# Moving the split weights to other byte offsets in SBUF

## The chip, the cores and the metric

The kernel runs on one core of a Trainium2 chip. The metric is the device time of one execution in microseconds (us). An instruction's duration is given in nanoseconds (ns). The engines are named as the profile names them: PE is the matrix engine (its weight loads are listed apart, as PEld), DVE the vector engine, ACT the scalar engine, POOL the GpSimd engine, and SP the engine that issues most of the transfers.

## What is computed

One layer of a transformer block on 512 rows of 1024 features, in float32: half a SwiGLU feed-forward added to the input, then a token mixer (four heads of differential attention and eight heads of dilated attention), then another half feed-forward, and a last normalisation.

```python
x = x + 0.5 * swiglu(rmsnorm(x, ffn1_norm), ffn1_w_gate, ffn1_w_up, ffn1_w_down)
x = x + token_mixer(rmsnorm(x, mix_norm), w_in, w_out, ...)
x = x + 0.5 * swiglu(rmsnorm(x, ffn2_norm), ffn2_w_gate, ffn2_w_up, ffn2_w_down)
return rmsnorm(x, final_norm)
```

The hidden width of the feed-forward is 2816, which is 22 blocks of 128. `w_in` is 1024 x 3072 (queries, keys and values of both kinds of heads), `w_out` is 1024 x 1024.

## The kernel before, in words

Activations are kept transposed: a tile has 128 features as partitions and the 512 rows as columns. PE multiplies in a format with fewer bits than float32 (fp32r), so each operand is split into a high and a low part, and `mm3` (lines 122 to 125) issues three matmuls for one product: high weight by high activation (line 123), high weight by low activation (line 124), low weight by high activation (line 125). Every matmul loads its stationary operand, 128 columns of 4 bytes, with a load of its own (LDWEIGHTS), and then streams its moving operand of 512 or 256 columns.

The split weights lie in one tile `w_all` of 6 x 1024 floats and a few more (line 100). `w_place(shift)` (line 103) deals out three places in turn: place i has its high part at column 1024 i + shift and its low part 3072 columns further on. `load_w` fetches raw weights into one of three `raw` buffers and takes a place. `split_w`, or `high` and `low`, then fill it: ACT casts the raw weights to the high part, DVE subtracts to get the low part. The program's framework makes each writer wait until the last matmul that read any column it overwrites has finished.

Three kinds of work use the places.

- Plain units: gate and up blocks at the start of each feed-forward, and the first six blocks of each down product. Their shift is 0, the matmuls are 512 columns wide, and the weights are the stationary operand.
- Units of seven products (function `pipeline` in `ffn`): the rest of the gate, up and down products is done two blocks by two, with seven products of half-size blocks in place of eight. Their shift is `ODD`, which is 8 floats or 32 bytes (the inner `high`, line 376). One product is twelve matmuls of 256 columns, the weights are the stationary operand, and the moving tiles start at multiples of 256 bytes. The first feed-forward has 23 such units and the second 25, so there are 48 x 7 = 336 products, or 4032 matmuls. Their order on PE, ACT and DVE is set by a heap of due times with a fixed step of 1410 ns for a product (`STEP`).
- The mixer: `load` (line 849) calls `load_w` with shift 0. Query and key products (`pq`, `pk`: 384 matmuls) and the output product (`pwo`: 192) stream 512 columns of activations over stationary weights. The value product (`pv`, lines 896 to 898: 384 matmuls) is the other way round: the activations are stationary, and 256 columns of the weights are the moving operand.

In the built program `w_all` starts at a multiple of 256 bytes, and so do all activation tiles. Therefore both operands of a value matmul start at the same place within 256 bytes, and the weights of a seven-product matmul stand 32 bytes past its moving operand. The three `raw` buffers, the first input tile and the small tiles are allocated behind `w_all`.

In the mixer the order on PE, ACT and DVE is written out by hand in chunks, with score, transpose and value work of the attention set between them. The output product is the end of the mixer: `wo_mm(m, ks)` multiplies output block m for the feature blocks `ks`. Blocks 3 to 7 are done whole, one after the other (line 1195), each in the order of k from 0 to 7, and `wo_end(m)` adds the result to the residual. The second feed-forward begins with plain units, whose weights (`raw_gub`) are split while the last output blocks are multiplied.

Of the kernel before, what the change touches and what calls it, by code (L numbers as in the profile page):

```python
# [15 lines left out]
F32R = mybir.dt.float32r  # L16
# [5 lines left out]
P = 128  # L22
# [3 lines left out]
KD = D // P  # L26
# [27 lines left out]

STEP, PLAIN_STEP = 1410, 4080
HS = S // 2
ODD = 8
F32_MAX = 3.4028234e38
PSUM = bass.MemoryType.PSUM
DRAM = bass.MemoryType.DRAM  # L60
# [4 lines left out]
def tile_macaron(ctx: ExitStack, tc, xs, xT, wf, wgu1, wst1, wd1, wdg1, wqk, wv, wo, wgu2, wst2, wd2,  # L65
# [8 lines left out]
    wp = ctx.enter_context(tc.tile_pool(name="wp", bufs=3))  # L74
# [7 lines left out]
    def mm_bank(nm):  # L82
        return pp.tile([P, S], F32, tag="mm", name=nm, bufs=4)
# [13 lines left out]

    w_all = wp.tile([P, 6 * 1024 + ODD], F32R, tag="w", name="w", bufs=1)  # L100
    w_used = [0]

    def w_place(shift=0):
        o = w_used[0] % 3 * 1024 + shift
        w_used[0] += 1
        return w_all[:, o:o + 1024], w_all[:, 3072 + o:4096 + o]

    def load_w(src, nm, n=1024, shift=0):
        raw = wp.tile([P, 1024], F32, tag="raw", name=f"raw_{nm}")
        nc.sync.dma_start(raw[:, :n], src)  # L110
        return (raw, *w_place(shift))
# [10 lines left out]
    def mm3(po, wh, wl, mh, ml, first, last, on=False):  # L122
        T.matmul(po, wh, mh, start=first, stop=False, skip_group_check=on)  # L123
        T.matmul(po, wh, ml, start=False, stop=False, skip_group_check=on)  # L124
        T.matmul(po, wl, mh, start=False, stop=last, skip_group_check=on)  # L125
# [72 lines left out]
    def ffn(wgu, wst, wd, wdg, n0, n1, norm, early, res, nm, hooks, ended, first=None,  # L198
# [169 lines left out]
        def high(t):  # L368
# [5 lines left out]
            else:  # L374
                if not half:
                    h, l = w_place(ODD)
                    half.extend([(h[:, :512], l[:, :512]), (h[:, 512:], l[:, 512:])])
# [231 lines left out]
        def pipeline():  # L609
            seen = {}  # L610
            for t, (u, o) in enumerate(ops):
                if o[0] == "p":
                    at(starts[t] - 2 * PLAIN_STEP, 1, load, u)
                    at(starts[t] - 3 * STEP, 3, high, t)
                    at(starts[t] - 2 * STEP, 2.5, low, t)
                else:
                    if t == begin[u]:
                        if u != units[0]:

                            time, s0 = starts[t] - 14 * STEP, sum_slots(u)  # L620
                            if s0 in seen:
                                time = max(time, starts[begin[seen[s0]] + 2])
                            seen[s0] = u
                            if u == ("g", PLAIN + 10):


                                time += STEP
                            at(time, 1, weight_sums, u)
                        at(starts[t] - 7 * STEP, 1.5, load, u)
                    if o[0] in ("s2", "s4"):  # L630
                        at(starts[t] - 5 * STEP, 2, total, t)
                    at(starts[t] - 4 * STEP, 3, high, t)
                    at(starts[t] - 3 * STEP, 2.5, low, t)
                at(starts[t], 4, product, t)
# [75 lines left out]
    with tc.manual_schedule(engines={mybir.EngineType.DVE, mybir.EngineType.Activation}):  # L710
        for t in range(4):
            raw = wp.tile([P, 1024], F32, tag="raw", name=f"raw_f{t}")
            h, l = w_place()
            for kk in range(2):
                k = 2 * t + kk
# [17 lines left out]
                for j in range(2):  # L733
                    for c in range(2):
                        o = kk * 512 + (2 * j + c) * P
# [104 lines left out]
    units, chunks = [], []  # L840
# [6 lines left out]
    loaded, ready, later = {}, {}, []  # L847

    def load(n):
        if n < len(units) and n not in loaded:  # L850
            loaded[n] = load_w(*units[n])
            ready[n] = loaded[n][1:]

    def high(n, c):
# [8 lines left out]
    def prep(n, now=False):  # L863
        if n >= len(units):
            return
        load(n)
        for c in (0, 512):
            if now:
                split_w(*loaded[n], c, c + 512)
            else:  # L870
                later.append((lambda c=c: high(n, c), lambda c=c: low(n, c)))
# [108 lines left out]
    mh, ml = [None] * KD, [None] * KD  # L980
# [147 lines left out]
    wo_ps = {}  # L1128

    def wo_mm(m, ks):  # L1130
        wh, wl = ready[wo_units[m]]
        for k in ks:
            o = k * P
            mm3(wo_ps[m][:], wh[:, o:o + P], wl[:, o:o + P], mh[k][:], ml[k][:],
                k == 0, k == KD - 1)

    def wo_chunk(m, c):
        if c == 0:
            if m + 2 < WO:
                prep(wo_units[m] + 2)  # L1140
            wo_ps[m] = mm_bank(f"pwo{m}")
        wo_mm(m, range(2 * c, 2 * c + 2))

    for m in range(WO):
        chunks += [lambda m=m, c=c: wo_chunk(m, c) for c in range(3)]
    chunks += [lambda m=m: wo_mm(m, [KD - 2]) for m in range(WO)]

    means, spread = rstd("n2", held)
# [31 lines left out]
    def wo_end(m):  # L1180
        V.tensor_tensor(x[m], wo_ps[m][:], x[m], op=ALU.add)
        split_x(m, 2, early[0][m], early[1][m])
        square_x(m)

    early = early_x("b")
    for m in range(WO):
        wo_mm(m, [KD - 1])
# [3 lines left out]
    for m in range(WO, KD):  # L1191
        if m > WO:
            prep(wo_units[m], True)
        wo_ps[m] = mm_bank(f"pwo{m}")
        wo_mm(m, range(KD))
        wo_end(m)

    eps = sp.tile([P, 1], F32, tag="eps", name="eps", bufs=1)
# [172 lines left out]
```

## Time and profile before

| | |
|---|---|
| median of three runs | 949.8 us (949.75 to 950.12) |
| span of the profiled execution | 950.1 us |
| PE busy | 934.4 us, 98% |
| weight loads busy | 866.6 us, 91% |
| DVE busy | 724.2 us, 76% |
| ACT busy | 533.0 us, 56% |

The profile gives the span of the profiled execution from its first to its last instruction; it gives no other time of that execution. A matmul's listed duration contains the time until its last result has left the array, which overlaps the next matmuls; the spacing from one start to the next is what a matmul costs. The first feed-forward's units of seven products run from about 84 to 349 us, the mixer from 349 to 598 us, and the second feed-forward from there to about 933 us.

### The profile page before, as it was taken

The numbers are of one execution on the slowest core, as the hardware profiler recorded it, in microseconds if no ns is written. First come the engines' busy times: TensorE is split into PE (matmuls) and PEld (weight loads), VectorE is DVE, ScalarE is ACT, GpSimd is POOL, SyncE is SP. The second block draws the span as 40 slices with busy tenths as digits, with TensorE's granted clock in tenths as the row PEclk, the third lists the DMA queues.
The fourth block names the chain that finished last, engine by engine and source line by source line (L and its number), as shares of the span: only waits on it lengthen the run. The fifth ranks groups of instructions, "written<-read, shape, count | busy, mean of one in ns | idle before, by whom it ended". The sixth has DMA issues, their size and how long they took to land.

```text
span 950.1 us, 17200 instructions
## 1 busy us (share of the span) xinstructions
PE 934.4 (98%) x6452; PEld 866.6 (91%) x6452; DVE 724.2 (76%) x1490; ACT 533.0 (56%) x1102; POOL 98.2 (10%) x117
## 2 busy tenths in 40 slices
PE   9999999999999999999999999999999999999995
PEld 7789999999999998988989888889999899999995
DVE  6697897777997896669764537697899677798786
ACT  7454664455664665566756645455666344666462
POOL 0011101012102100000000003201110111220100
PEclk9999999999999999999999999999999999999997
DMA  7176646578757642443232204454673857874732
GB/s 249 62 202 153 156 128 177 143 192 204 189 147 184 180 129 67 132 134 117 83 113 89 67 23 133 132 148 119 157 205 89 209 142 181 223 190 118 194 106 89
DMA packets 60388, 136.71 MB, mean 144 GB/s; under 512 B 6848, under 2 KB 9152, under 8 KB 60304
## 3 DMA queue, kind: packets, MB, share of 16 engines
q1 hardware_dynamic: 46304, 110.14, 35.3%
q0 software_dynamic: 14000, 25.47, 17.1%
q8 instruction: 50, 0.82, 0.4%
q14 instruction: 34, 0.28, 0.1%
HBM read 130.30 MB, written 2.14 MB: 139 GB/s over the span
## 4 chain that ended last, share of the span: by engine, by line
PE 91%; DVE 5%; ACT 1%; issue 1%; DMA 1%; SPq 0%; DVEq 0%
PE po L1038 2%; PE pwo L123 1%; PE pwo L124 1%; PE pwo L125 1%; PE pua L123 1%; PE pua L124 1%; PE pua L125 1%; PE pv L898 1%; PE pv L896 1%; PE pv L897 1%; PE pt L1025 1%; PE pq L123 1%; PE pq L125 1%; PE pq L124 1%; PE pdb L125 1%; PE pdb L124 1%
## 5 line engine op out<-in xcount | busy, mean ns | idle before, releaser
L1004 DVE CUSTOM_DVE_ANT_0 pr<-sc,strip 128x128 f32<-128x128 f32 (+3 forms) x64 | 30.9, 488 | 35.1 <-PE sc L1002 34.8
L1007 ACT ACTIVATE pr<-pr,mx 128x128 f32<-128x128 f32 (+3 forms) x64 | 36.0, 563 | 32.5 <-DVE mx L1004 31.6
L382 ACT CAST w<-s2b 128x512 fp32r<-128x512 f32 x50 | 31.0, 620 | 17.6 <-DVE s2b L364 14.4
L386 DVE TENSOR_TENSOR w<-s2b,w 128x512 fp32r<-128x512 f32 x50 | 34.2, 685 | 8.0 <-ACT w L382 7.9
L382 ACT CAST w<-s2a 128x512 fp32r<-128x512 f32 x46 | 28.6, 621 | 18.7 <-DVE s2a L364 15.7
L1038 PEld LDWEIGHTS po<-v,ptb 128*128 128x128 f32 x240 | 32.8, 191 | 5.3 <-ACT ptb L1028 2.7
L150 POOL TENSOR_TENSOR sq<-sq,sqt 128x512 f32<-128x512 f32 x7 | 10.9, 1557 | 254.7 <-ACT sqt L149 254.7
L386 DVE TENSOR_TENSOR w<-s2a,w 128x512 fp32r<-128x512 f32 x46 | 31.5, 684 | 6.6 <-ACT w L382 6.5
L896 PE MATMUL pv<-w,xh 128*128 128x256 f32 x128 | 36.2, 283 | 0.0
L898 PE MATMUL pv<-w,xh 128*128 128x256 f32 x128 | 36.2, 283 | 0.0
L897 PE MATMUL pv<-w,xl 128*128 128x256 f32 x128 | 36.2, 282 | 0.0
L1038 PE MATMUL po<-v,ptb 128*128 128x64 f32 (+1 forms) x240 | 32.6, 269 | 1.8 <-ACT ptb L1028 1.7
L1028 ACT COPY ptb<-pt 128x128 f32<-128x128 f32 (+3 forms) x48 | 20.1, 424 | 20.2 <-PE pt L1025 19.9
L123 PE MATMUL pq<-xh,w 128*128 128x512 f32 x64 | 26.9, 421 | 0.0
L123 PE MATMUL pwo<-mh,w 128*128 128x512 f32 x64 | 26.1, 408 | 0.0
L124 PE MATMUL pwo<-ml,w 128*128 128x512 f32 x64 | 25.5, 398 | 0.0
L125 PE MATMUL pwo<-mh,w 128*128 128x512 f32 x64 | 25.5, 398 | 0.0
L124 PE MATMUL pq<-xl,w 128*128 128x512 f32 x64 | 25.1, 393 | 0.0
L123 PE MATMUL pk<-xh,w 128*128 128x512 f32 x64 | 25.1, 392 | 0.0
L125 PE MATMUL pq<-xh,w 128*128 128x512 f32 x64 | 25.1, 392 | 0.0
L125 PE MATMUL pk<-xh,w 128*128 128x512 f32 x64 | 25.0, 391 | 0.0
L124 PE MATMUL pk<-xl,w 128*128 128x512 f32 x64 | 25.0, 390 | 0.0
(661 smaller groups left out, 3990.0 us busy)
## 6 DMA issues: line engine op xcount, KB each, us to landing
raw_qk<-wqk_dram SPq DMA_DIRECT2D x16, 512.0 KB, 3.3
raw0bg<-wst_dram SPq DMA_DIRECT2D x9, 512.0 KB, 4.5
raw_gua<-wgu_dram SPq DMA_DIRECT2D x8, 512.0 KB, 3.9
raw0ag<-wst_dram SPq DMA_DIRECT2D x8, 512.0 KB, 4.7
raw0ad<-wdg_dram SPq DMA_DIRECT2D x8, 512.0 KB, 4.5
strip<-bias_rows SPq DMA_DIRECT2D x16, 256.0 KB, 3.6
raw_v<-wv_dram SPq DMA_DIRECT2D x8, 512.0 KB, 3.3
raw_wo<-wo_dram SPq DMA_DIRECT2D x8, 512.0 KB, 3.2
```

Source lines behind the costliest of these rows:

```text
L123: T.matmul(po, wh, mh, start=first, stop=False, skip_group_check=on)
L124: T.matmul(po, wh, ml, start=False, stop=False, skip_group_check=on)
L125: T.matmul(po, wl, mh, start=False, stop=last, skip_group_check=on)
L382: A.copy(made[t][0], source(t))
L386: V.tensor_tensor(l, source(t), h.bitcast(F32), op=ALU.subtract)
L896: T.matmul(po, xh[k][:, xs], wh[:, o:o + 256], start=k == 0, stop=False)
L897: T.matmul(po, xl[k][:, xs], wh[:, o:o + 256], start=False, stop=False)
L898: T.matmul(po, xh[k][:, xs], wl[:, o:o + 256], start=False, stop=k == KD - 1)
L1004: V.tensor_tensor_reduce(out=pi, in0=ps[:, :w], in1=st["b"][m][:, w - 1::-1], op0=ALU.add, op1=ALU.min, scale=1.0, scalar=3.0e38, accum_ou ...
L1007: A.activation(pi, pi, AF.Exp, scale=-1.0, bias=st["mx"][:, m, i:i + 1], accum_out=st["ls"][:, m, i:i + 1])
L1028: A.copy(ptb[:, :w], pt[:, :w])
L1038: T.matmul(st["po3"][:, i, d0:d0 + dn], st["ptb", m, i][:, k * P:(k + 1) * P], vt[u // 4, k][:, fo + d0:fo + d0 + dn], start=k == 0, stop= ...
```

## The change

The shift of the units of seven products goes from 8 to 13 floats (52 bytes), and the mixer's units get a shift of 51 floats (204 bytes, which is 52 short of 256). `w_all` grows by 43 floats. The last output block goes through k from 7 to 0 in place of 0 to 7; which matmul opens and which closes the sum in PSUM is set accordingly.

```diff
-ODD = 8
+ODD = 13
+MIX = 51
...
-    w_all = wp.tile([P, 6 * 1024 + ODD], F32R, tag="w", name="w", bufs=1)
+    w_all = wp.tile([P, 6 * 1024 + MIX], F32R, tag="w", name="w", bufs=1)
...
     def load(n):
         if n < len(units) and n not in loaded:
-            loaded[n] = load_w(*units[n])
+            loaded[n] = load_w(*units[n], shift=MIX)
...
     def wo_mm(m, ks):
         wh, wl = ready[wo_units[m]]
-        for k in ks:
+        for n, k in enumerate(ks):
             o = k * P
-            mm3(wo_ps[m][:], wh[:, o:o + P], wl[:, o:o + P], mh[k][:], ml[k][:],
-                k == 0, k == KD - 1)
+            first, final = (n == 0, n == KD - 1) if len(ks) == KD else (k == 0, k == KD - 1)
+            mm3(wo_ps[m][:], wh[:, o:o + P], wl[:, o:o + P], mh[k][:], ml[k][:], first, final)
...
-        wo_mm(m, range(KD))
+        wo_mm(m, range(KD)[::-1] if m == KD - 1 else range(KD))
```

In the built program the tiles behind `w_all` move up by 192 bytes (the `raw` buffers from 32 to 224 bytes past a multiple of 256). The matmuls on PE are the same and stand in the same order, but for the last output block. On ACT and DVE the same instructions stand in another order at two places: at the beginning of the mixer the first two casts of `raw_qk` stand behind the last copy of `pyda`, and at its end the two first splits of `raw_gub` change places, so that the one which overlaps the last 51 columns of the last output block's weights comes second.

## The prediction

> **What bounds the kernel now.** I read the page's shares first, then the chain that ended last, then busy time by stage, and then single matmuls, because the change touches only where their operands lie.
>
> ```profile
> span 950.1 us, 17200 instructions
> ...
> PE 934.4 (98%) x6452; PEld 866.6 (91%) x6452; DVE 724.2 (76%) x1490; ACT 533.0 (56%) x1102; POOL 98.2 (10%) x117
> ...
> PEclk9999999999999999999999999999999999999997
> ...
> PE 91%; DVE 5%; ACT 1%; issue 1%; DMA 1%; SPq 0%; DVEq 0%
> ```
>
> PE is busy 98% of the span and is 91% of the chain. The granted clock is full nearly everywhere, so the throttle is no part of this. The windows by stage (first feed-forward's units of seven products, mixer, second feed-forward) say where PE has slack:
>
> ```profile
> 84.00:349.00 265.00, 264.70 (x2088) 257.27 (x2087) 216.09 (x402) 153.45 (x309) 37.65 (x45) 1.00 0.65 167
> 349.00:598.00 249.00, 245.64 (x1491) 217.25 (x1490) 158.60 (x433) 145.79 (x353) 9.12 (x6) 0.99 0.31 98
> 598.00:933.00 335.00, 335.00 (x2474) 319.24 (x2473) 271.46 (x503) 186.77 (x365) 45.16 (x51) 1.00 0.60 155
> 700.00:740.00 40.00, 40.00 (x340) 40.00 (x339) 35.13 (x67) 25.46 (x54) 3.48 (x4) 1.00 0.50 132
> ```
>
> The columns are the window, its length, and busy us of PE, PEld, DVE, ACT and POOL. PE has 0.3, 3.4 and 0.0 us of idle time in the three stages. So what one matmul costs is paid in full, times the number of matmuls. The busiest stretch of DVE that I looked at has it at 35.13 of 40 us; it has room for a PE that is some per cent faster.
>
> **What one matmul costs now.** The spacing of starts is the cost. From the timeline of PE, three pairs of rows: a stretch of products of seven (the second row is 120 matmuls after the first), a value product (16 after), and the last output block with the first matmul behind it (24 after).
>
> ```profile
> 178.67 0.28 PE L123 MATMUL pxda<-h5a,w 128*128 128x256 f32 x1
> ...
> 192.87 0.28 PE L123 MATMUL pxda<-h5a,w 128*128 128x256 f32 x1
> ```
> ```profile
> 362.80 0.28 PE L898 MATMUL pv<-w,xh 128*128 128x256 f32 x1
> ...
> 364.72 0.28 PE L896 MATMUL pv<-w,xh 128*128 128x256 f32 x1
> ```
> ```profile
> 592.28 0.39 PE L123 MATMUL pwo<-mh,w 128*128 128x512 f32 x1
> ...
> 597.72 0.39 PE L123 MATMUL pgb<-ehb,w 128*128 128x512 f32 x1
> ```
>
> 14.20 us / 120 = 118.3 ns in the products of seven; 1.92 us / 16 = 120.0 ns in the value product; 5.44 us / 24 = 226.7 ns at 512 columns. The first two have the same shape, 128x128 weights and 256 columns. They differ by 1.7 ns, in every such stretch, as the groups show:
>
> ```profile
> L124 PE MATMUL pwgb<-xl,w 128*128 128x256 f32 x72 | 20.2, 281 | 0.0
> L898 PE MATMUL pv<-w,xh 128*128 128x256 f32 x128 | 36.2, 283 | 0.0
> L125 PE MATMUL pk<-xh,w 128*128 128x512 f32 x64 | 25.0, 391 | 0.0
> ```
>
> The listed duration is the spacing plus about 163 ns (281 against 118.3, 283 against 120.0), so differences of durations are differences of cost. Per operation, with least, median and largest duration:
>
> ```profile
> L124 PE MATMUL pwgb<-xl,w x72: 277/281/285, 654.1 to 868.7; 128*128 128x256 f32 x72
> ...
> L125 PE MATMUL pk<-xh,w x64: 388/389/398, 349.7 to 536.5; 128*128 128x512 f32 x64
> ```
> ```profile
> L898 PEld LDWEIGHTS pv<-w,xh x128: 187/192/192, 362.0 to 516.9; 128*128 128x128 f32 x128
> L898 PE MATMUL pv<-w,xh x128: 278/283/288, 362.1 to 517.0; 128*128 128x256 f32 x128
> ```
>
> In the products of seven the offset between the two operands is 32 bytes (modulo 256), in the value product it is 0. The weight loads differ too: 192 ns at offset 0, against 188 in the products of seven:
>
> ```profile
> L124 PEld LDWEIGHTS pwgb<-xl,w x72: 187/188/191, 654.0 to 868.6; 128*128 128x128 f32 x72
> ```
>
> I read this as the load of the next weights and the stream of this matmul getting into each other's way, more at offset 0 than at 32.
>
> **The change part by part.**
>
> *Products of seven, 32 to 52 bytes.* 48 units x 7 products x 12 = 4032 matmuls. No row has an offset of 52. Bounds: if every one took the least duration (277 in place of 281) the stage would win 4 x 4032 = 16.1 us, if every one took the largest (285) it would lose 16.1 us. I take the slope between the two offsets that the trace has: 1.67 ns for 32 bytes, so another 1.04 ns for 20 bytes. That is 4032 x 1.04 = 4.2 us less, a spacing of 117.3 ns.
>
> *Value product, weights 0 to 204 bytes.* Here the weights are the moving operand. The stationary tile is then 204 bytes behind, which modulo 256 is 52 ahead, the same relation as above. By the same slope 52 x 0.052 = 2.7 ns; 384 x 2.7 = 1.0 us less. Bounds: least 278 against 283, 1.9 us less; largest 288, 1.9 us more. The stage has PE idle of 3.4 us in all, so most of it reaches the end.
>
> *Query, key and output products, 0 to 204 bytes at 512 columns.* 384 + 192 matmuls. The load is done well inside the stream of 512 columns. Taken at 0; bounds from the key row: least 388 against a mean of 391, 576 x 3 = 1.7 us less; largest 398, 4.0 us more.
>
> *Casts and subtractions to the new places, raw buffers 192 bytes higher.* Taken at 0, because the offsets of the trace make no difference to them and PE covers them:
>
> ```profile
> L382 ACT CAST w<-s2b 128x512 fp32r<-128x512 f32 x50 | 31.0, 620 | 17.6 <-DVE s2b L364 14.4 <-PE pyub L125 1.4 <-PE pdb L125 1.0
> L114 ACT CAST w<-raw_qk 128x512 fp32r<-128x512 f32 x4 | 2.5, 620 | 1.9 <-DVE lp L806 0.9 <-PE pwda L124 0.5 <-ACT w L382 0.5
> ```
>
> The first writes 32 bytes past, the second 0, both 620 ns. If they grew 5%, DVE would stand at 36.9 of 40 us in the window above, still behind PE.
>
> *Seam into the mixer.* A place at shift 51 covers the head of the next place, so the casts of `raw_qk` wait for three more matmuls (3 x 118 = 0.35 us), and the first one also stands behind the copy of `pyda`.
>
> ```profile
> 342.97 0.62 ACT L114 CAST w<-raw_qk 128x512 fp32r<-128x512 f32 x1 [0.45 <-ACT w L382]
> 343.50 0.37 ACT L411 COPY pyda<-pxda 128x256 f32<-128x256 f32 x1
> 344.40 0.63 ACT L114 CAST w<-raw_qk 128x512 fp32r<-128x512 f32 x1 [0.53 <-PE pwda L124]
> 345.97 0.62 ACT L114 CAST w<-raw_qk 128x512 fp32r<-128x512 f32 x1 [0.95 <-DVE lp L806]
> ...
> 349.81 0.62 ACT L787 ACTIVATE sqd<-x 128x512 f32<-128x512 f32 x1
> ```
> ```profile
> 348.52 0.40 PE L123 MATMUL pq<-xh,w 128*128 128x512 f32 x1
> ```
>
> The first query matmul starts at 348.52, over 4 us after the first cast, so it doesn't wait. Queued behind the third cast on ACT are a table load and the squares (349.81) that the normalisation of the mixer waits for; these may come up to 0.35 us later, and the chain goes through them. I take 0.3 us more, with 0 and 0.4 as ends.
>
> *Seam into the second feed-forward.* Its first split (`raw_gub`) now overlaps the last 51 columns of the last output block, so it must wait for block k = 7. The reversed order of k puts that first: three matmuls, until 592.28 + 0.68 = 592.96 (without the reversal: 597.72, a stall of PE for the cast). ACT casts both `raw_gub` tiles from 592.25 on, 1.05 us each, DVE subtracts at 1.23 each:
>
> ```profile
> 592.25 1.05 ACT L114 CAST w<-raw_gub 128x1024 fp32r<-128x1024 f32 x1 [3.24 <-PE pwo L124]
> ```
> ```profile
> 593.33 1.23 DVE L115 TENSOR_TENSOR w<-raw_gub,w 128x1024 fp32r<-128x1024 f32 x1 [0.17 <-ACT w L114]
> ```
>
> Done by about 595.9, before PE wants them at 597.72: 0 us.
>
> ```profile
> 587.89 1.23 DVE L115 TENSOR_TENSOR w<-raw_gub,w 128x1024 fp32r<-128x1024 f32 x1 [0.17 <-ACT w L114]
> ```
> ```profile
> 603.13 1.05 ACT L114 CAST w<-raw_gub 128x1024 fp32r<-128x1024 f32 x1 [3.24 <-PE pub L124]
> ```
>
> The buffer of the first tile is free now when its subtraction ends, at 589.1, and will be at 595.9, so the load after it is issued that much later. The cast that this load serves is the fourth and starts at 603.13; I take the 7 us left as enough.
>
> **Sum** against the profiled execution: 950.1 - 4.2 - 1.0 + 0.3 = 945.2. Its span is 0.3 us over the median of the runs, so 944.9 for the median.
>
> **The rivals.**
>
> *Slower: 52 bytes is a worse place than 32.* The slope is drawn through two points. [...] It decides as soon as the mean spacing rises by 0.2 ns, where it eats the 1.0 - 0.3 us of the other parts. [...]
>
> *No change: the offset is not what separates the two.* The value product also swaps the roles of weights and activations. If that makes the 1.7 ns, the offset does nothing and only the seam is left: 949.8 + 0.3 = 950.1. For it: all groups of the products of seven agree at 281 whatever their tiles. Against it: both have the same shapes and the loads differ too. [...]
>
> **How the numbers follow.** A measurement of this kernel can tell about 0.2%, 1.9 us. Faster, as forecast: 0.62. Slower through the spacing: 0.26; through a seam or a slower 512-column stream (up to 4.0 us): 0.03. No change: 0.09. So faster 0.62, same 0.09, slower 0.29. The range: at the low end the spacing falls by 2.5 of the possible 4 ns (10.1 us), the value product wins 1.9 and the seam costs nothing, 949.8 - 12.0 = 937.8; at the high end the slower rival, 956.8. Cases of both signs hold much of the chance; the forecast's own range is 937.8 to 947.5.
>
> **What would show it.** Right: the groups of 256-column matmuls at about 280 in the products of seven and 280 in place of 283 in the value product, loads of 188 there, 512-column groups unchanged, PE still at 98%. Wrong: groups at 283 or more, or at 281 with the value product alone moved; idle time of PE at the start of the second feed-forward or before the mean of squares at the start of the mixer.

## The result, and the profile after

The changed kernel takes 955.5 us (median of four runs, 954.04 to 955.67); the kernel before, run beside it, 949.8 us. The ratio is 1.0047, with a 95% interval of 1.0034 to 1.006: slower by 0.47%. The prediction said 944.9 us and faster.

The page of the kernel after: span, busy time by engine, granted clock, and the chain that ended last.

```profile
span 953.8 us, 17198 instructions
...
PE 938.2 (98%) x6452; PEld 868.2 (91%) x6452; DVE 726.0 (76%) x1490; ACT 533.5 (56%) x1102; POOL 97.4 (10%) x117
...
PEclk9999999999999999999999999999999999999998
...
PE 91%; DVE 5%; ACT 1%; issue 1%; DMA 0%; SPq 0%; DVEq 0%
```

The shape is that of before: the same number of matmuls, PE at 98%, the granted clock full nearly everywhere (a mean of 0.995, before 0.993). The windows by stage of the kernel after (the same columns as before: window, length, busy us of PE, PEld, DVE, ACT, POOL) show hardly any new idle time:

```profile
84.00:349.00 265.00, 264.45 (x2091) 256.99 (x2090) 217.05 (x408) 154.29 (x311) 37.74 (x45) 1.00 0.63 168
349.00:598.00 249.00, 245.61 (x1482) 214.99 (x1481) 158.68 (x426) 144.53 (x350) 8.15 (x6) 0.99 0.30 94
598.00:933.00 335.00, 335.00 (x2443) 319.21 (x2442) 269.34 (x498) 184.78 (x360) 45.19 (x51) 1.00 0.60 157
```

PE is idle for 0.6, 3.4 and 0.0 us, against 0.3, 3.4 and 0.0 before. What moved is the number of matmuls that a window holds: 2091 against 2088 in the first, 1482 against 1491 in the mixer, 2443 against 2474 in the second feed-forward. So single matmuls cost something else than before, and not the same in both feed-forwards. The timeline of PE in the kernel after, two pairs of rows, the first 132 matmuls apart, the second 120:

```profile
106.50 0.28 PE L124 MATMUL pzua<-txa,w 128*128 128x256 f32 x1
...
121.46 0.28 PE L124 MATMUL pxga<-txa,w 128*128 128x256 f32 x1
...
655.08 0.28 PE L124 MATMUL pwgb<-xh,w 128*128 128x256 f32 x1
...
669.48 0.28 PE L124 MATMUL pwgb<-xh,w 128*128 128x256 f32 x1
```

14.96 us / 132 = 113.3 ns in a part of the first feed-forward; 14.40 us / 120 = 120.0 ns in the second. Before it was 118.3 ns in every long run. The same shape, the same 52 bytes and the same code now have two prices, one on each side of the old one. From the start of every matmul in the trace: of 336 products (twelve matmuls each) 266 take 1440 ns, which is 120.0 ns a matmul, and 43 take 1360 ns, which is 113.3. The cheap ones lie at 105 to 153 us and 313 to 334 us, all in the first feed-forward; every long run of products in the second is dear. Nine products take 1412 to 1415 ns, seven of them in a row at 338 to 348 us, so a third spacing of about 117.8 ns occurs too. In the kernel before, 276 of 336 take 1420 ns, with the rest mostly 1415 and 1425.

The groups by tile (least, median, largest duration in ns) say the same. Of the kernel after, a gate product of the second feed-forward, one of the first, a key product and a value product:

```profile
L125 PE MATMUL pwgb<-xl,w x72: 283/283/283, 655.2 to 872.5; 128*128 128x256 f32 x72
...
L125 PE MATMUL pwga<-xl,w x64: 276/283/283, 84.7 to 279.6; 128*128 128x256 f32 x64
...
L125 PE MATMUL pk<-xl,w x64: 388/397/419, 348.4 to 536.1; 128*128 128x512 f32 x64
...
L898 PE MATMUL pv<-w,xl x128: 278/279/285, 361.0 to 516.4; 128*128 128x256 f32 x128
```

The gate product stands at exactly 283 in the second feed-forward (281 before) and has 276 beside 283 in the first. The key product went from 389 to 397, the value product from 283 to 279.

By stages, from the first matmul of each, after against before: the units of seven products and what lies between them in the first feed-forward 262.86 against 263.66 us (0.8 less), the mixer 251.34 against 249.19 (2.1 more), the second feed-forward up to the last matmul 346.76 against 343.78 (3.0 more), the head 0.2 less. That makes 4.1 us at the last matmul; behind it 0.4 us is given back, and the spans differ by 3.7. Both executions contain a dip of the granted clock in the mixer, of which the last section tells. Not all executions do, which is the likely reason why the medians differ by 5.7 us and not by 3.7. It also means that the profiled execution of before was no middle one: this one of after took 955.55 us at a span of 953.8, so a span lies some 1.8 us under the time, the span of 950.1 us belongs to about 951.9 us, and the 0.3 us that the prediction allowed between span and median was too simple.

### The profile page after: what moved, and what is told of

Its sections match the earlier page's. It is cut to its first block, busy times and chain, and to the rows that moved or that the text cites. A ratio compares the mean times of both kernels' runs of the same rounds, so it can differ in the third digit from the quotient of the medians.

```text
span 953.8 us, 17198 instructions
## 1 busy us (share of the span) xinstructions
PE 938.2 (98%) x6452; PEld 868.2 (91%) x6452; DVE 726.0 (76%) x1490; ACT 533.5 (56%) x1102; POOL 97.4 (10%) x117
## 4 chain that ended last, share of the span: by engine, by line
PE 91%; DVE 5%; ACT 1%; issue 1%; DMA 0%; SPq 0%; DVEq 0%
PE po L1039 2%; PE pwo L124 1%; PE pwo L125 1%; PE pwo L126 1%; PE pua L124 1%; PE pua L125 1%; PE pua L126 1%; PE pq L126 1%; PE pv L898 1%; PE pv L899 1%; PE pv L897 1%; PE pq L124 1%; PE pq L125 1%; PE pt L1026 1%; PE pk L125 1%; PE pk L126 1%
```

## The experiments

All ratios are to the kernel before, run on the same chip. "Products" are the products of seven, twelve matmuls of 256 columns each. Their counts come from one profiled execution of each kernel. Some of the changed kernels vary more from one execution to the next than the kernel before (954.4 to 959.1 us with an extra matmul of 256 columns, 948.4 to 953.8 us at 48 bytes with one of 64; the kernel before at most 949.7 to 952.0), so in other executions the runs of products may have fallen otherwise.

**Each half of the change alone.** The 52 bytes without the mixer's shift and without the reversed last block:

```diff
-            loaded[n] = load_w(*units[n], shift=MIX)
+            loaded[n] = load_w(*units[n])
-        wo_mm(m, range(KD)[::-1] if m == KD - 1 else range(KD))
+        wo_mm(m, range(KD))
```

> Only the shift of the units of seven products changes (32 to 52 bytes); the mixer keeps shift 0 and the old order of k, and the raw buffers stand where the changed kernel has them. Theory A (at 52 bytes the spacing of 256-column matmuls has two steady values, 113.3 and 120.0 ns, that is 1360 and 1440 ns for a product; which one a run of products falls into is decided by how PE enters it): the same mixture as in the changed kernel, the second feed-forward at 1440 throughout, so about 1.9 us less than the changed kernel, which is what the mixer lost by the difference of the two traces: 953.5 us. Theory B (the offset in the mixer or the moved raw buffers slow the products of seven): products back at 1420, about 950 us.

Measured: 952.5 us, ratio 1.0030 (1.0019 to 1.0041). 266 products at 1440 ns and 48 at 1360. Gate products of the second and first feed-forward in this run:

```profile
L125 PE MATMUL pwgb<-xl,w x72: 283/283/283, 652.3 to 869.6; 128*128 128x256 f32 x72
...
L125 PE MATMUL pwga<-xl,w x64: 276/283/283, 85.6 to 280.4; 128*128 128x256 f32 x64
```

The same two prices in the same places as in the kernel after, but for the last products of the first feed-forward: the mixer has no part in them. The other half, `ODD = 8` with `MIX = 51` and the reversal:

> Only the mixer's shift (204 bytes, with the reversed last output block); the units of seven products stay at 32 bytes. Theory A: products at 1420 ns as before, value matmuls at 117.5 ns, 512-column matmuls of the mixer slower than before by 3 to 6 ns, so 949.8 + 1.9 = 951.7 us. Theory B: products of seven slower than 1420 ns because the raw buffers moved, up to 1440: 949.8 + 1.9 + 6.7 = 958.

Measured: 953.1 us, ratio 1.0026 (1.0016 to 1.0037). A gate product, the value and a key product of this run:

```profile
L125 PE MATMUL pwgb<-xl,w x72: 277/281/285, 654.4 to 869.0; 128*128 128x256 f32 x72
...
L898 PE MATMUL pv<-w,xl x128: 277/279/285, 361.7 to 517.2; 128*128 128x256 f32 x128
...
L125 PE MATMUL pk<-xl,w x64: 388/397/419, 349.1 to 536.8; 128*128 128x512 f32 x64
```

The products of seven stay at 1420 ns (282 of 336), though the `raw` buffers stand where the kernel after has them: the moved buffers do not slow them. Summing the spacings of these two runs, neither of which has the dip of the clock: the value product falls from 46.57 to 46.01 us (0.6 less), while the 512-column matmuls rise: `pk` 45.23 to 45.99, `pq` 46.03 to 46.72, `pwo` 46.35 to 47.60, together 2.7 more. The reversal of the last output block has no visible part in that: the block takes 5.63 us, the three ahead of it 5.64 or 5.65, and all four 5.44 at shift 0. The mixer goes from 247.67 to 249.80 us, 2.1 more. So both halves lose, by 0.30% and 0.26%, and within their intervals they add up to the 0.47% of the whole. The 0.26% may be in part the dip of the clock: the profiled execution of this run, which has none, took 951.5 us, the seven others 952.8 to 953.4 us at a mean clock of 0.993 to 0.995 in place of 0.996.

**Offset or roles.** `ODD = 0`, mixer as before:

> The units of seven products at shift 0, all else as before (raw buffers as in the changed kernel). If the offset makes the 1.7 ns between the products of seven and the value product (premise of the prediction): 120.0 ns a matmul, 1440 ns a product, 949.8 + 6.7 = 956.5 us. If the exchanged roles of weights and activations make it: 118.3 ns, 1420, 949.8 us.

Measured: 956.6 us, ratio 1.0068 (1.0053 to 1.0083). 319 products at 1440 ns; the gate product of the second feed-forward:

```profile
L125 PE MATMUL pwgb<-xl,w x72: 283/283/283, 655.0 to 872.4; 128*128 128x256 f32 x72
```

Without an offset the products cost the 120.0 ns of the value product. The offset makes the 1.7 ns; that weights and activations swap their roles does not.

**What chooses between the two prices.** In the kernel after, a run of products that follows directly on 512-column matmuls is dear (all six of them). The cheap ones follow an interruption of PE, be it a short wait, as at 103.66 us, or four matmuls of another product (`pbias`), as at 310.91 us. A third interruption, at 334 to 336 us, is followed by the seven products at 1412 to 1415 ns. The timeline at the first:

```profile
102.98 0.28 PE L124 MATMUL pxga<-tta,w 128*128 128x256 f32 x1
103.10 0.28 PE L125 MATMUL pxga<-tta,w 128*128 128x256 f32 x1
103.21 0.28 PE L126 MATMUL pxga<-tta,w 128*128 128x256 f32 x1
103.66 0.38 PE L124 MATMUL pyga<-xh,w 128*128 128x256 f32 x1 [0.16 <-DVE rbc_n L415]
```

From this I formed a new theory: at 52 bytes the stream of 256-column matmuls has two steady spacings, and how PE enters a run decides which of them it keeps. To change the entry alone, one extra matmul of 64 columns stands ahead of each run of products that follows 512-column matmuls (six places). The product behind it starts its bank anew, so the extra result is overwritten.

```diff
+            if t == 0 or ops[t - 1][1][0] == "p":
+                T.matmul(banks[o[1]][:, :64], h[:, :P], moving(u, o[2])[0][0][:, :64],
+                         start=True, stop=True, skip_group_check=True)
```

> The changed kernel with one matmul of 64 columns more wherever a run of products of seven begins behind 512-column matmuls (six places, about 0.1 us each); its result is overwritten by the matmul behind it. Theory A: the entry is another, so whole runs of products change over between 1440 and 1360 ns; if all of them do, some 270 products x 80 ns = 21.6 us less than the changed kernel, 934 us; if none does, 956 us. Theory B' (transfers and the other engines' traffic set the spacing): no product changes its pace, 956 us.

Measured, on top of the kernel after: 935.4 us, ratio 0.9844 (0.9829 to 0.9859). 293 products at 1360 ns. The timeline of PE in this run, the entry and two rows 120 matmuls apart:

```profile
646.32 0.39 PE L126 MATMUL pub<-xh,w 128*128 128x512 f32 x1
646.55 0.19 PE L445 MATMUL pwgb<-xh,w 128*128 128x64 f32 x1
646.58 0.36 PE L124 MATMUL pwgb<-xh,w 128*128 128x256 f32 x1
...
648.06 0.28 PE L124 MATMUL pzgb<-txb,w 128*128 128x256 f32 x1
...
661.66 0.28 PE L124 MATMUL pygb<-txb,w 128*128 128x256 f32 x1
```

13.60 us / 120 = 113.3 ns. Six small matmuls take 20 us off the kernel after. Two controls: the same extra matmul in the kernel before (32 bytes), and one of 256 columns in the kernel after.

> The kernel before (32 bytes, mixer at 0) with the same six matmuls of 64 columns. Theory A (the spacing has two steady values at 52 bytes, chosen by the entry): in the trace of before, runs of products come back to 1420 ns after every interruption, so at 32 bytes there is only one; no gain, 950.2 + 0.5 = 950.7 us. Rival C (an extra short matmul helps by itself, at any offset): products at 1360 ns, some 930 us.

> The changed kernel with an extra matmul of 256 columns in place of 64. Theory A: the extra matmul now is like one more matmul of the product, so the run is entered as in the changed kernel and falls into 1440 ns at the same places: 955.5 + 0.7 = 956.2 us. Rival C: as with 64 columns, 935 us.

At 32 bytes: 951.0 us, ratio 1.0003 (0.9994 to 1.0013); products still at 1415 to 1425 ns. At 52 bytes with 256 columns: 958.0 us, ratio 1.0074 (1.0057 to 1.0091); 271 products at 1440 ns (the profiled execution took 954.4 us; what makes the others longer is not known). The gate product of the second feed-forward in the one and in the other:

```profile
L124 PE MATMUL pwgb<-xl,w x72: 277/281/286, 652.6 to 867.4; 128*128 128x256 f32 x72
```
```profile
L125 PE MATMUL pwgb<-xl,w x72: 284/284/284, 653.7 to 871.2; 128*128 128x256 f32 x72
```

So an extra matmul as such gains nothing, and at 32 bytes there is nothing to gain by the choice: 1415 and 1425 ns take turns, 1420 in the mean as before. The gain takes both: the offset of 52 bytes in place of 32, and an entry that differs from an even stream. Which property of the small matmul makes the entry good, its width, its length in time or the change of widths, was not varied beyond 64 and 256 columns.

**A better kernel.** 52 bytes in the products, the 64-column entry, and the mixer as it was before:

> 52 bytes in the units of seven products, the extra matmul of 64 columns, and the mixer as before (shift 0, old order of k). Theory A: products at 1360 ns as with the extra matmul in the changed kernel, and the mixer without what shift 204 cost it (1.9 to 2.7 us): 932.5 to 933.5 us. If the mixer's shift does not matter here: 935.4 us.

Measured: 934.6 us (932.9 to 935.04), ratio 0.9820 (0.9806 to 0.9835), the fastest of all. 274 products at 1360 ns; 21 at 1440, all between 307 and 342 us, in a stretch that begins after an interruption and not behind 512-column matmuls. That interruption is the one by the four `pbias` matmuls, behind which the kernel after had 1360 ns: an interruption by itself does not settle the spacing. Then 52 bytes everywhere, the plain units and the mixer too, with the 64-column entry:

> All split weights 52 bytes past, in the plain units and the mixer too, with the extra matmul of 64 columns. [...] If 512-column matmuls fall into a slow value at 52 bytes, as in the mixer at 204 (231 to 238 ns against 226.7): up to 2016 x 7 = 14 us more, 947 us. [...]

Measured: 941.3 us, ratio 0.9896 (0.9878 to 0.9914). Plain up products of the kernel with 52 bytes in the products alone, and of this one:

```profile
L125 PE MATMUL pub<-xl,w x24: 389/389/389, 626.2 to 646.6; 128*128 128x512 f32 x24
...
L125 PE MATMUL pub<-xl,w x24: 392/392/393, 631.3 to 652.3; 128*128 128x512 f32 x24
```

The mean spacing of the plain down products rises from 227.0 to 233.2 ns, that of the up products from 226.9 to 233.3: about twice the 3 ns of the listed durations, so at 512 columns a difference of durations is not the difference of cost. So an offset costs a 512-column matmul: 6.2 ns here at 52 bytes, 2.7 us / 576 = 4.7 ns at 204 bytes in the mixer. For them the aligned places are the good ones. At last, the extra matmul at the start of all 48 units, in place of the six places:

```diff
-            if t == 0 or ops[t - 1][1][0] == "p":
+            if t == begin[u] or ops[t - 1][1][0] == "p":
```

> 52 bytes, mixer at 0, with the extra 64-column matmul at the start of each of the 48 units (its result is overwritten) in place of the 6 places behind 512-column matmuls. If the extra matmul only ever helps into the spacing of 113.3 ns: the run of about 20 products near 307 to 341 us leaves 1440 for 1360 within one unit, 1.2 us less, against 42 more small matmuls of 30 to 60 ns, 1.3 to 2.5 us more: ratio 0.982 to 0.984. If it can also throw a run at 113.3 back to 120.0 ns: many products at 1440 and a ratio of 0.988 or more.

Measured: 937.9 us, ratio 0.9866 (0.9849 to 0.9882), between the two that I had put down. No long run is left at 1440 ns and none was thrown back, but the first product of a unit takes 1452 ns in place of 1360. An extra matmul in mid-stream thus costs 92 ns, more than the 30 to 60 that I had put down, and 42 x 92 ns = 3.9 us is more than the 1.2 us won.

**Is it the multiple of 16?** 0 and 32 bytes, where one spacing was the rule, are multiples of 16, and 52 is not. 48 and 64 bytes in the products, each without an extra matmul, and 48 with it; the mixer as before.

> Shift of the units of seven products at 12 floats (48 bytes, a multiple of 16) in place of 13, mixer at 0, order of the last output block as before. If two steady spacings (113.3 and 120.0 ns) belong to a range of offsets around 52 bytes, the products stand mostly at 1440 ns after 512-column matmuls, as with 52 bytes alone, and the ratio to before is about 1.003. If the slower state at 52 comes from its not being a multiple of 16 bytes, 48 bytes has one spacing below 118.3 ns, by the prediction's slope 117.5 ns (1410 ns a product), and the ratio is about 0.996 or less.

> Shift of the units of seven products at 16 floats (64 bytes), otherwise as the run at 48 bytes. Two spacings for a range of offsets: mostly 1440 ns a product or a mix with 1360, ratio 0.99 to 1.004. Multiples of 16 bytes as the cause: one spacing, by the prediction's slope 116.7 ns (1400 ns a product), ratio about 0.993.

> 48 bytes with the extra 64-column matmul where products begin behind 512-column matmuls (its result is overwritten), mixer at 0. If 48 bytes has the same two spacings as 52: nearly all products at 1360 ns, ratio about 0.982 as at 52 bytes. If 48 has one spacing like 32 bytes: the extra matmul changes nothing against 48 bytes alone.

Measured: 48 bytes 951.4 us, ratio 1.0003 (0.9994 to 1.0013), 266 products at 1420 ns; 64 bytes 946.8 us, ratio 0.9961 (0.9946 to 0.9976), 303 products at 1413 or 1414 ns and 15 at 1360; 48 bytes with the extra matmul 949.8 us, ratio 0.9997 (0.9983 to 1.0011), 258 products at 1413 or 1414 and 50 at 1420. Two rows of the timeline 120 matmuls apart, at 64 bytes:

```profile
651.93 0.28 PE L124 MATMUL pwgb<-xh,w 128*128 128x256 f32 x1
...
666.06 0.28 PE L124 MATMUL pwgb<-xh,w 128*128 128x256 f32 x1
```

14.13 us / 120 = 117.8 ns. 64 bytes with the extra matmul was not run. Several spacings at one offset are therefore no speciality of 52 bytes: 48 bytes has 118.3 and 117.8 ns (and a run of six products at 1480 ns, 123.3 a matmul), 64 bytes has 117.8 and 113.3. Neither theory was right as I had written it: two prices as far apart as 120.0 and 113.3 were not seen at 48 bytes, and multiples of 16 do not have one spacing each. What sets the list of spacings at an offset stays open. One thing more stands in the traces: from matmul to matmul, a spacing is the mean of a round that repeats. In the second feed-forward the starts are 120 ns apart each time at 0 bytes; 122, 118, 117, 121, 116, 116, 120 and 117 ns at 32 (to within 1 ns, and the same round with the extra matmul); 118, 122 and 120 in the dear runs at 52 (119, 121 and 120 in 54 products of the kernel after, from 766 to 845 us), and 113 or 114 each time in the cheap ones.

## Why the prediction was wrong

*Products of seven, 4.2 us less.* This is the step that failed. I drew a slope of 0.052 ns per byte through 0 bytes (120.0 ns) and 32 bytes (118.3) and read 117.3 at 52. There is no slope: 0, 32, 48, 52 and 64 bytes gave mostly 120.0, 118.3, 118.3, 120.0 and 117.8 ns, and 52 bytes has 113.3 as well. The mean over the kernel after came out above that of before because 266 products of 336 entered the dear spacing: the products won 0.7 us in the first feed-forward and lost 3.3 in the second, 2.6 us more where 4.2 less was forecast. The bounds of 16.1 us to both sides held for the kernel after, and the lower one was near what another entry gives: in the run with the 64-column entry the groups stand at 276, one below the least of before, and the products take 17.6 us less than before. The row "277/281/285" had shown that the price is not one value; its spread is the round of eight spacings above, a pattern and not scatter around a slope, and I had used it only for bounds.

*Value product, 1.0 us less.* Right in sign, 0.6 us in size (a median of 117 ns in place of 120, a mean of 119.8 in place of 121.3). That the sign was right is luck, since it came from the same slope. The relation of 52 bytes, which costs 120.0 or 113.3 ns in the products of seven, costs about 118 ns here. The offset modulo 256 alone does not set the price.

*512-column matmuls, 0.* Wrong in size: 2.7 us more, within the bounds of 1.7 less to 4.0 more. The reason given, that the load of the weights is done well inside a long stream, did not help: the loads of `pk` take 188 ns in the median as before, less than the 226.7 ns spacing of the last output block before, yet the largest durations of its matmuls rise from 397 to 419. This term alone turns the mixer's part of the change into a loss.

*Casts, 0.* Held: the group of the page after has 622 ns against 620, and PE has no new idle time in the second feed-forward.

```profile
L383 ACT CAST w<-s2b 128x512 fp32r<-128x512 f32 x50 | 31.1, 622 | 17.8 <-DVE s2b L365 14.7
```

*Seam into the mixer, 0.3 us more.* Not borne out; that the idle time rose by about this much is chance. The cast of `raw_qk` did fall behind the copy of `pyda` and did wait for PE, as the timeline of ACT in the kernel after shows:

```profile
342.02 0.36 ACT L412 COPY pyda<-pxda 128x256 f32<-128x256 f32 x1 [0.52 <-PE pxda L126]
342.30 0.62 ACT L115 CAST w<-raw_qk 128x512 fp32r<-128x512 f32 x1
343.67 0.62 ACT L115 CAST w<-raw_qk 128x512 fp32r<-128x512 f32 x1 [0.75 <-PE pyda L125]
```

PE's idle time in the first of the three windows rose by 0.25 us. But the one new wait of PE from 335 to 365 us is for an addition to the residual ahead of the mixer, not what I had named (waiter, what it waited for, us in total, times, longest):

```profile
PE pyda L124 <- DVE x L424: 0.4, 1, 0.4
```

The two halves settle it. With 52 bytes alone, where the seam is as before, the same wait is there (0.37 us); with the mixer's shift alone, where the casts wait as in the kernel after, it is not, and the first feed-forward takes 263.64 us against 263.66 before. So the seam cost nothing, and the wait came with the products' new spacing.

*Seam into the second feed-forward, 0.* Held: the last output matmul starts at 598.58 us and the first gate matmul at 598.81, one spacing later, and PE is busy for all of the window behind.

*The rivals.* The first, that 52 bytes is a worse place than 32, stood at 956.8 us: 949.8, the 0.3 of the seam, and 4032 x 1.67 ns = 6.7 us for products back at 120.0 ns; 955.5 was measured. Its number was right for four products in five. No run shows 6.7 us as a price of 52 bytes: in the kernel after 266 products stood at 120.0 ns and 43 at 113.3, and in the run with the 64-column entry 293 stood at 113.3, against 118.3 at 32 bytes. The second, that the offset does nothing, fell with the run at 0 bytes: places alone moved the spacing from 118.3 to 120.0 ns. My reading of the first rows, that the load of the next weights and the running stream get into each other's way, stays a guess. The loads of the gate products in the second feed-forward take 192 ns in the median in the run at 0 bytes and 188 at 32; at 52 bytes one of the three groups takes 193 and two take 188 in the kernel after, and all three 188 in the run with the 64-column entry. So the longer loads go with the dear spacing, and which of the two makes the other, no run shows. Of the ranges, 937.8 and 956.8 us are worked out; the 947.5 us at the upper end of the forecast's own range is not.

## What to carry to other kernels

Two points are no slope: where a cost per instruction spreads within one group (277/281/285), look at the sequence of single spacings and find what puts the stream into one pattern or another before pricing a new point between them. A layout change is worth trying together with a change of the entry into the stream, since here the same 52 bytes alone were 0.3% slower, or 1.8% faster, and six matmuls that compute nothing decided it. And an offset that helps one shape should stay with that shape: 512-column matmuls paid 5 to 6 ns for it.

## What the runs showed of the hardware that I had not expected

A steady stream keeps its spacing for long. At 52 bytes runs of 83 products, about 1000 matmuls, stayed at 1440 ns each, and runs of 46 at 1360; behind 512-column matmuls, a single 64-column matmul at the start decided which. 113.3 ns is half of the 226.7 ns of a 512-column matmul at offset 0, so at that spacing the 256-column matmuls lose nothing per column against the long ones, and 120.0 ns is 6.7 ns of loss in each. What sets the loss, and why the entry is remembered, no run here shows.

Half the clock after a wait of 1.7 us. In the mixer PE waits that long for ACT; in some executions six 512-column matmuls behind it then take 427 to 574 ns in place of 227, 1.2 us or more in all. The timeline of the kernel after, and a window over that place (the first number behind the engines is the granted clock, 0.56; from 544.0 to 547.3 us alone it is 0.50):

```profile
543.13 1.26 PE L1039 MATMUL po<-v,ptb 128*128 128x64 f32 x8 [1.67 <-ACT ptb L1029]
544.14 0.78 PE L124 MATMUL pwo<-mh,w 128*128 128x512 f32 x1
```
```profile
543.50:547.00 3.50, 3.50 (x14) 2.92 (x14) 2.03 (x4) 0.74 (x2) 0.00 (x0) 0.56 0.07 25
```

The profiled executions with 52 bytes alone and with the mixer's shift alone have the same wait and no dip. Seven of the fourteen traces have it, each for 3.41 us and beginning 0.8 to 2.0 us after the end of this wait, and from 10 to 920 us none shows another dip; that the wait brings it on is argued from this place, since no run changed the wait. Why the dip comes in some executions only, no run shows.
